# A hybrid decoder layer: seven block products for eight in the up-projection, and a down-projection of its own

## The chip, the cores and the metric

The kernel runs on one core of one Trainium2 chip. The metric is device time in microseconds (us) of one execution; the kernel before takes 2393.1 us (median of three runs, 2392.64 to 2393.7). Engines: PE does matmuls (PEld is its weight load), DVE is the vector engine, ACT the scalar engine, POOL is GpSimd and SP issues most DMA transfers (SPq, POOLq: their queues).

## What is computed

One layer on 2048 tokens of 1024 features. First a token-mixing part (retention, short convolution and an output projection), which the change leaves alone. Then the part that it rebuilds:

```python
h = modulate(rms_norm(x, norm2_g[layer]), shift2, scale2)
up = h @ w_up[layer]                    # 1024 -> 2 x 2816
a, val = up[..., :D_FF], up[..., D_FF:]
a = causal_dwconv(a, ffn_conv_w[layer]) + ffn_conv_b[layer]
ffn = (jax.nn.silu(a) * val) @ w_down[layer]     # 2816 -> 1024
x = x + gate2[:, None, :] * ffn
```

A last modulated norm gives the output. All tensors are float32.

## The kernel before

Features lie on the 128 partitions, tokens along the free dimension in blocks of 512 (four blocks; 8 feature chunks of 128). Every matmul operand is kept as two parts in the format fp32r, the rounded value and the rest (`split_act` at L217 for tokens, `split_w` at L83 for weights: an ACT cast, then a DVE subtraction). A product takes three matmuls for each 128 x 128 weight block (`mm3`, L235: value x value, value x rest, rest x value).

The token-mixing part runs over the four blocks. Its output projection (`out_proj`, L474) writes the residual x1 of each block to DRAM (`x1d`, stored by POOL's queue) and sums its squares; `norm2` (L497) turns the sum into the row `r2d`, also in DRAM. Between the steps of `out_proj` small jobs are placed by `spread` (L608): the next token chunks, and `more_mod` (L596), which reduces conditioning weights on DVE (L166). During the last output projection the 8 chunks of block 0 for the second part are made by `h2_chunk` (L684: load, a DVE multiplication, an ACT scaling, a split), and those of block 1 follow.

The second part works on 1024 tokens at a time (B = 0, 1; two blocks s). For each of 22 column chunks j of 128 it computes gate and value (`Up.a` L723, `Up.v` L739): 24 matmuls each into one of four PSUM banks `mm`, for each s. ACT copies the gate out of PSUM, then come the three-tap convolution (L731 to L733), Silu (L736), the product with the value (L744) and the split into g, which stays in SBUF. After every second j `down_part` (L752) multiplies two g chunks with two chunks of w_down and adds the result to the residual tiles `acc` in SBUF (L759), for 8 output chunks m and both s; the four PSUM banks sc0, sc1, y, misc take turns. At the end of B = 0 the last four chunks of the down-projection go in two groups, and after each m one token chunk of the next 1024 tokens is made (L866 to L874), so these lie between matmuls:

```python
for js in ((j - 3, j - 2), (j - 1, j)):
    ws = [get_w("w_down", q) for q in js]
    for m in range(KC):
        for s in range(2):
            down_part([gs[q] for q in js], ws, acc, s, m)
        if js[1] != j:
            hs[0].append(h2_chunk(2, m, r_s, new_xm()))
        else:
            hs[1].append(h2_chunk(3, m, r_t, new_xm()))
```

At the end of B = 1 the last four chunks go for blocks of 512, 256 and 256 tokens, so that the final norm and the stores (`Final`, L761) of one block lie beside the matmuls of the next; only the last 256 tokens are left behind the last matmul.

Each engine works through its queue in order. Outside `tc.manual_schedule()` the framework's planner sets the order of each queue: the instructions in the order of the program, but one that is not ready can be passed by later ones. Waits come from data and from buffers: a pool gives a tag a number of buffers (`bufs`), and a tile waits until the tile that had its buffer is done with. Weights are loaded through 3 raw buffers and split into 4 buffers, in the order of `plan` and up to `ahead` tiles early (`get_w`, L110).

## Time and profile before

| what | before |
|---|---|
| median of 3 runs | 2393.1 us |
| the profiled execution | 2391.5 us |
| its span, first to last instruction | 2389.7 us |
| PE busy | 2357.0 us (99%) |
| DVE busy | 1495.0 us (63%) |
| ACT busy | 838.1 us (35%) |
| moved by DMA | 239.5 MB, mean 100 GB/s |

The profile is that of one execution. Its span runs from the first to the last instruction and is 1.8 us shorter than that execution's time. Busy times overlap, as the engines work side by side. In rows by line, "mean ns" is what one instruction takes by itself; instructions of one engine follow each other a little closer than that, since the end of one overlaps the start of the next. "Clock" is the share of TensorE's full speed that was granted.

### The profile page before, as it was taken

The numbers are of one execution on the slowest core, as the hardware profiler recorded it, in microseconds if no ns is written. First come the engines' busy times: TensorE is split into PE (matmuls) and PEld (weight loads), VectorE is DVE, ScalarE is ACT, GpSimd is POOL, SyncE is SP. The second block draws the span as 40 slices with busy tenths as digits, with TensorE's granted clock in tenths as the row PEclk, the third lists the DMA queues.
The fourth block names the chain that finished last, engine by engine and source line by source line (L and its number), as shares of the span: only waits on it lengthen the run. The fifth ranks groups of instructions, "written<-read, shape, count | busy, mean of one in ns | idle before, by whom it ended". The sixth has DMA issues, their size and how long they took to land.

```text
span 2389.7 us, 27984 instructions
## 1 busy us (share of the span) xinstructions
PE 2357.0 (99%) x10954; PEld 1951.6 (82%) x10954; DVE 1495.0 (63%) x2755; ACT 838.1 (35%) x1234; POOL 32.0 (1%) x67
## 2 busy tenths in 40 slices
PE   8999999999999999999999999999999999999997
PEld 5888888888888887888888888888888888888887
DVE  8999759866986688644444444448844444444436
ACT  5255325523552355322222222235622222222234
POOL 0000000000000000000000000000100000000000
PEclk9999999999999999999999999999999999999998
DMA  8444633554264328311111111112511111111101
GB/s 308 144 132 135 230 111 112 175 189 150 71 217 153 115 84 271 103 53 53 40 50 53 53 39 50 53 53 72 189 58 45 44 53 53 44 45 53 53 27 71
DMA packets 88660, 239.53 MB, mean 100 GB/s; under 512 B 10240, under 2 KB 12304, under 8 KB 88528
## 3 DMA queue, kind: packets, MB, share of 16 engines
q1 hardware_dynamic: 84096, 223.71, 28.6%
q0 software_dynamic: 4288, 13.91, 1.5%
q8 instruction: 86, 1.41, 0.2%
q14 instruction: 46, 0.38, 0.0%
q10 hardware_dynamic: 144, 0.13, 0.0%
HBM read 219.88 MB, written 17.83 MB: 99 GB/s over the span
## 4 chain that ended last, share of the span: by engine, by line
PE 61%; issue 28%; DVE 6%; DMA 2%; ACT 1%; POOL 1%; SPq 0%; POOLq 0%; DVEq 0%; ACTq 0%
PE mm L237 14%; PE mm L238 14%; PE mm L239 14%; PE sc L239 3%; PE sc L238 3%; PE sc L237 3%; PE misc L237 2%; PE y L238 2%; PE y L239 2%; PE y L237 2%; PE misc L238 2%; PE misc L239 2%; DMA x<-in_x 1%; DVE mw L166 1%; DVE w L89 1%
## 5 line engine op out<-in xcount | busy, mean ns | idle before, releaser
L237 PE MATMUL mm<-act,w 128*128 128x512 f32 x2048 | 801.1, 391 | 1.3 <-DVE xr L492 1.1
L238 PE MATMUL mm<-act,w 128*128 128x512 f32 x2048 | 797.7, 389 | 1.0 <-DVE act L219 1.0
L239 PE MATMUL mm<-act,w 128*128 128x512 f32 x2048 | 797.3, 389 | 0.0
L88 ACT CAST w<-raw 128x1024 fp32r<-128x1024 f32 x271 | 282.9, 1051 | 656.6 <-issue 352.2
L237 PEld LDWEIGHTS mm<-act,w 128*128 128x128 f32 x2048 | 384.5, 188 | 81.4 <-ACT act L218 2.6
L238 PEld LDWEIGHTS mm<-act,w 128*128 128x128 f32 x2048 | 384.6, 188 | 80.7 <-DVE act L219 2.1
L239 PEld LDWEIGHTS mm<-act,w 128*128 128x128 f32 x2048 | 384.4, 188 | 80.4
L89 DVE TENSOR_TENSOR w<-raw,w 128x1024 fp32r<-128x1024 f32 x271 | 328.9, 1222 | 120.6 <-ACT w L88 120.6
L237 PE MATMUL mm<-w,act 128*128 128x512 f32 x480 | 187.9, 393 | 6.5 <-ACT act L218 3.6
L238 PE MATMUL mm<-w,act 128*128 128x512 f32 x480 | 188.0, 392 | 0.0
L239 PE MATMUL mm<-w,act 128*128 128x512 f32 x480 | 186.6, 391 | 0.0
L759 DVE SCALAR_TENSOR_TENSOR acc<-sc,mod,acc 128x512 f32<-128x512 f32 (+1 forms) x172 | 126.8, 738 | 76.7 <-PE sc L239 76.6
L732 DVE SCALAR_TENSOR_TENSOR fi<-a,cp,fi 128x512 f32<-128x512 f32 x88 | 66.1, 752 | 172.4 <-ACT fi L731 172.4
L744 DVE TENSOR_TENSOR fi<-fi,mm 128x512 f32<-128x512 f32 x88 | 60.5, 688 | 168.0 <-PE mm L239 167.3
L729 ACT COPY a<-mm 128x512 f32<-128x512 f32 x88 | 51.7, 588 | 315.2 <-PE mm L239 315.2
L238 PE MATMUL sc<-g,w 128*128 128x512 f32 (+1 forms) x348 | 132.9, 382 | 0.0
L237 PE MATMUL sc<-g,w 128*128 128x512 f32 (+1 forms) x348 | 132.8, 382 | 0.0
L239 PE MATMUL sc<-g,w 128*128 128x512 f32 (+1 forms) x348 | 132.8, 382 | 0.0
L237 PEld LDWEIGHTS mm<-w,act 128*128 128x128 f32 x480 | 90.0, 188 | 29.5 <-ACT act L218 9.6
L239 PEld LDWEIGHTS mm<-w,act 128*128 128x128 f32 x480 | 90.6, 189 | 19.3 <-DVE act L219 0.2
L238 PEld LDWEIGHTS mm<-w,act 128*128 128x128 f32 x480 | 90.7, 189 | 18.9 <-DVE w L542 0.5
L735 DVE COPY ah<-a 128x2 f32<-128x2 f32 x44 | 7.4, 169 | 156.2 <-ACT a L729 156.2
(226 smaller groups left out, 2812.9 us busy)
## 6 DMA issues: line engine op xcount, KB each, us to landing
raw<-in_w_up SPq DMA_DIRECT2D x88, 512.0 KB, 3.6
raw<-in_w_tok SPq DMA_DIRECT2D x64, 512.0 KB, 5.2
x<-in_mod_w SPq DMA_DIRECT2D x96, 256.0 KB, 4.1
raw<-in_w_conv SPq DMA_DIRECT2D x48, 512.0 KB, 3.5
raw<-in_w_down SPq DMA_DIRECT2D x44, 512.0 KB, 3.5
raw<-in_w_out SPq DMA_DIRECT2D x32, 512.0 KB, 3.5
x<-in_x SPq DMA_DIRECT2D x56, 256.0 KB, 3.9
mw<-in_mod_w SPq DMA_DIRECT2D x32, 256.0 KB, 4.6
```

Of the source, the lines that this page charges most:

```text
L88: S.copy(w[:, 0, :], raw)
L89: V.tensor_tensor(w[:, 1, :], raw, w[:, 0, :].bitcast(F32), op=ALU.subtract)
L166: V.scalar_tensor_tensor(raw, raw, 1.0, half, op0=ALU.mult, op1=ALU.mult, accum_out=part[:, q : q + 1])
L237: T.matmul(out, lhs[0], rhs[0], start=first, stop=False)
L238: T.matmul(out, lhs[0], rhs[1], start=False, stop=False)
L239: T.matmul(out, lhs[1], rhs[0], start=False, stop=last)
L729: S.copy(at[:, 2 + o : 514 + o], pa)
L732: V.scalar_tensor_tensor(cv, at[:, 1 + o : 513 + o], fcw[:, j, 1:2], cv, op0=ALU.mult, op1=ALU.add)
L735: V.tensor_copy(ah[:, j, :], at[:, 512 + o : 514 + o])
L744: V.tensor_tensor(sl, sl, pv, op=ALU.mult)
L759: V.scalar_tensor_tensor(acc[s][m][:, cs], ps, gate_of(1, m), acc[s][m][:, cs], op0=ALU.mult, op1=ALU.add)
```

## The change

The up-projection of 1024 tokens and of one column chunk pair (gate A, value V) is seen as a product of 2 x 2 blocks: the feature halves are 1 (chunks 0 to 3) and 2 (chunks 4 to 7), the token halves are the two blocks. Instead of eight block products, seven of combined operands are made (12 matmuls of 512 columns each, `product`). The combinations of tokens H11, H21, H12, H22 (feature half, token half) are made once for 1024 tokens, in four chunks (`Tokens`): T1 = H12 - H11, T2 = H22 - T1, T3 = H22 - H12, T4 = H21 - T2. Those of the weights are made for each column chunk (`Weights`), from the same loads.

A chunk's products are `start` (A1 H11 and A2 H21: the gate of token half 1), `middle` (with T2, T1 and T3) and `finish` (with T4 and H22). The products with H11, T2, T3 and T4 add up in one bank `pb`; after the first three ACT copies the bank (`snap`), and the copies are the partial sums that the other outputs need. `finish` of a chunk comes after `start` of the next one.

Gate times value is no longer kept in SBUF: POOL's queue writes it to DRAM (`gd`). When the up-projection of all tokens is done, a stage of its own does the down-projection for five token blocks of 512, 512, 512, 256 and 256: for each of 22 chunks it loads and splits the weights and g, and adds into eight PSUM banks, one for each output chunk m; m = 7 lags three chunks. At a block's end each bank is added to the residual, loaded then from `x1d`. The four token chunks for the first 1024 tokens are made in and after the last output projection (two of the `more_mod` jobs go from there to the convolution stage before it), those for the second 1024 tokens where the loop reaches i = 22. The memory of each stage's buffers is that of the stage before.

```diff
--- before.py
+++ after.py
...
+    base, wts = ExitStack(), ExitStack()
+    actp = base.enter_context(tc.tile_pool(name="actp", bufs=16))
+    fo = base.enter_context(tc.tile_pool(name="fo", bufs=4))
...
+    sp = wts.enter_context(tc.tile_pool(name="sp", bufs=7, side="right"))
+    whlp = wts.enter_context(tc.tile_pool(name="whlp", bufs=4, side="right"))
+    rawp = wts.enter_context(tc.tile_pool(name="rawp", bufs=3, side="right"))
...
-    for B in range(2):
-        for j in range(FC):
-            plan += [("w_up", j), ("w_up", FC + j)]
-            if j % 2 == 0 and 2 <= j < FC - 2:
-                plan += [("w_down", j - 2), ("w_down", j - 1)]
-            if j == FC - 1:
-                plan += [("w_down", q) for q in range(j - 3, j + 1)]
...
                 ret[j + 1].scores()
-                if j == 0:
+                if j == 0 or b == NB - 1:
                     more_mod()
...
+    p1.close()
+    p2 = ExitStack()
+    act2 = p2.enter_context(tc.tile_pool(name="act2", bufs=12, reuse_waits="tile"))
+    p3 = ExitStack()
+    hx = p3.enter_context(tc.tile_pool(name="hx", bufs=1, reuse_waits="tile"))
...
+    def h2_f32(b, k, r, t):
+        nc.sync.dma_start(t, x1d[b][k])
+        V.tensor_tensor(t, t, r, op=ALU.mult)
+        S.activation(t, t, AF.Identity, bias=shift_of(1, k), scale=amul[:, 1, k : k + 1])
+        return t
...
+        def chunk(self, i):
+            X, b, r = self.X, self.b, self.r
+            h11 = h2_f32(b, i, r[0], self.tmp())
+            X["11"].append(split_into(new_act(), h11))
+            h21 = h2_f32(b, i + 4, r[0], self.tmp())
+            X["21"].append(split_into(new_act(), h21))
+            h12 = h2_f32(b + 1, i, r[1], self.tmp())
+            h22 = h2_f32(b + 1, i + 4, r[1], self.tmp())
+            V.tensor_tensor(h11, h12, h11, op=ALU.subtract)
+            t2 = self.tmp()
+            V.tensor_tensor(t2, h22, h11, op=ALU.subtract)
+            X["T2"].append(split_into(new_x2(), t2))
+            X["T1"].append(split_into(new_x2(), h11))
+            V.tensor_tensor(h12, h22, h12, op=ALU.subtract)
+            X["T3"].append(split_into(new_x2(), h12))
+            t4 = self.keep() if self.keep else t2
+            V.tensor_tensor(t4, h21, t2, op=ALU.subtract)
+            if self.keep:
+                self.t4.append(t4)
+            else:
+                X["T4"].append(split_into(new_act(), t4))
+                X["22"].append(split_into(new_act(), h22))
+        def late(self, i):
+            self.X["T4"].append(split_into(new_act(), self.t4[i]))
+            self.X["22"].append(split_into(new_act(), h2_f32(self.b + 1, i + 4, self.r[1], self.tmp())))
...
+    tk = Tokens(0, [load_r2(0, new_hx("r", 2)), load_r2(1, new_hx("r", 2))], ft, lambda: new_hx("t4", 4))
+    ss2 = out_proj(3, mixed, spread(cv[3].norm, lambda k: tk.chunk(k) if k < 4 else None))
...
+    for i in range(4):
+        tk.late(i)
+    norm2(3, ss2)
+    p3.close()
+    pf.close()
+    wts.close()
+    p4 = ExitStack()
+    ap_ = p4.enter_context(tc.tile_pool(name="ap_", bufs=2, reuse_waits="tile"))
+    p4.enter_context(tc.tile_pool(name="sp3", bufs=7, side="right")).tile([128, 8], F32, tag="s", name="sp3")
+    whlp = p4.enter_context(tc.tile_pool(name="whlp2", bufs=5, side="right", reuse_waits="tile"))
+    rawp = p4.enter_context(tc.tile_pool(name="rawp2", bufs=4, side="right", reuse_waits="tile"))
...
+        def one(self):
+            self.a = self.new()
+            self.split(self.a, slice(0, 1024), self.wa)
+        def two(self):
+            wa, wv = self.wa, self.wv
+            lo, hi = slice(0, 512), slice(512, 1024)
+            s12 = rawp.tile([128, 1024], F32, tag="raw", name=nm("raw"))
+            V.tensor_tensor(s12[:, lo], wv[:, lo], wv[:, hi], op=ALU.add)
+            V.tensor_tensor(s12[:, hi], s12[:, lo], wa[:, lo], op=ALU.subtract)
+            self.s = self.new()
+            self.split(self.s, slice(0, 1024), s12)
+            self.b = self.new()
+            self.split(self.b, lo, wv[:, hi])
+            V.tensor_tensor(wv[:, lo], wa[:, lo], wv[:, lo], op=ALU.subtract)
+            V.tensor_tensor(wa[:, hi], wa[:, hi], s12[:, hi], op=ALU.subtract)
+            self.split(self.b, hi, wa[:, hi])
+        def three(self):
+            self.c = fo.tile([128, 2, 512], F32R, tag="q", bufs=1, name=nm("q"))
+            self.split(self.c, slice(0, 512), self.wv[:, 0:512])
+    def product(ps, w, c0, x, first):
+        for i in range(4):
+            cs = slice(c0 + 128 * i, c0 + 128 * (i + 1))
+            mm3(ps, [w[:, q, cs] for q in range(2)], [x[i][:, q, :] for q in range(2)], first and i == 0, i == 3, True)
 
...
+        def snap(self):
+            t = ft_o() if self.n % 2 else fo.tile([128, 512], F32, tag="xr", name=nm("sn"))
+            self.n += 1
+            S.copy(t, self.pb)
+            return t
+        def gate_branch(self, s, part, ps):
+            j, at, o = self.j, self.at, 512 * s
+            V.tensor_tensor(at[:, 2 + o : 514 + o], part, ps, op=ALU.add)
+            cv = new_ss() if s == 0 else fo.tile([128, 512], F32, tag="xr", name=nm("cv"))
+            S.activation(cv, at[:, 2 + o : 514 + o], AF.Identity, bias=fcb[:, j : j + 1], scale=fcw[:, j, 2:3])
+            V.scalar_tensor_tensor(cv, at[:, 1 + o : 513 + o], fcw[:, j, 1:2], cv, op0=ALU.mult, op1=ALU.add)
+            V.scalar_tensor_tensor(cv, at[:, o : 512 + o], fcw[:, j, 0:1], cv, op0=ALU.mult, op1=ALU.add)
+            if s == 1:
+                V.tensor_copy(ah[:, j, :], at[:, 512 + o : 514 + o])
+            S.activation(cv, cv, AF.Silu)
+            return cv
...
+            self.pb, self.pg = ps_tag(("sc0", "sc1")[j % 2]), ps_tag(("y", "misc")[j % 2])
+            product(self.pb, w.a, 0, X["11"], True)
+            s1 = self.snap()
+            pa = ps_mm()
+            product(pa, w.a, 512, X["21"], True)
+            self.sl0 = self.gate_branch(0, s1, pa)
+        def middle(self):
+            X, w = self.X, self.w
+            product(self.pb, w.s, 512, X["T2"], False)
+            self.u2 = self.snap()
+            product(self.pg, w.s, 0, X["T1"], True)
+            product(self.pb, w.c, 0, X["T3"], False)
+            self.v1 = self.snap()
+            V.tensor_tensor(self.v1, self.v1, self.pg, op=ALU.add)
+        def finish(self):
+            X, w, B, j = self.X, self.w, self.B, self.j
+            product(self.pb, w.b, 0, X["T4"], False)
+            V.tensor_tensor(self.sl0, self.sl0, self.pb, op=ALU.mult)
+            nc.gpsimd.dma_start(gd[2 * B][j], self.sl0)
+            product(self.pg, w.b, 512, X["22"], False)
+            sl1 = self.gate_branch(1, self.u2, self.pg)
+            V.tensor_tensor(sl1, sl1, self.v1, op=ALU.mult)
+            nc.gpsimd.dma_start(gd[2 * B + 1][j], sl1)
...
+    for i in range(2 * FC):
+        B, j = divmod(i, FC)
+        if i == FC:
+            last.finish()
+            last = None
+            turn = [0]
+            def tmp():
+                turn[0] += 1
+                return ft_o() if turn[0] % 2 else fo.tile([128, 512], F32, tag="xr", name=nm("h"))
+            tk = Tokens(2, [load_r2(2, new_ss()), load_r2(3, new_ss())], tmp)
+            for c in range(4):
+                tk.chunk(c)
+        w = nxt
+        u = Up(B, j, w, tk.X)
+        more = i + 1 < 2 * FC
+        if more:
+            nxt = Weights((j + 1) % FC)
+        u.start()
+        if more:
+            nxt.raw()
+            nxt.one()
+        if last is not None:
+            last.finish()
+        if more:
+            nxt.two()
+        u.middle()
+        if more:
+            nxt.three()
+        last = u
+    last.finish()
...
+    whlp, gp, rawp, grp = pool("whlp3", 6), pool("gp", 6), pool("rawp3", 3), pool("grp", 4)
+    accp, fo, sp = pool("accp", 18), pool("fo2", 4), pool("sp2", 8)
+    BANKS = ("mm", "mm", "mm", "mm", "sc0", "sc1", "y", "misc")
+    LAG = 3
...
+        def evict(self, ps, m):
+            t = accp.tile([128, 512], F32, tag="acc", name=nm("acc"))[:, 0 : self.n]
+            b, o = divmod(self.t0, 512)
+            nc.sync.dma_start(t, x1d[b][m][:, o : o + self.n])
+            V.scalar_tensor_tensor(t, ps, gate_of(1, m), t, op0=ALU.mult, op1=ALU.add)
+            self.acc.append(t)
...
+    for t0, n in ((0, 512), (512, 512), (1024, 512), (1536, 256), (1792, 256)):
+        b, o = divmod(t0, 512)
+        fin = Final(t0, n)
+        ws, gs = {}, {}
+        ps = [None] * KC
+        def part(m, k):
+            if k == 0:
+                ps[m] = ps_tag(BANKS[m])[:, 0:n]
+            mm3(ps[m], [ws[k][:, q, 128 * m : 128 * (m + 1)] for q in range(2)],
+                [gs[k][:, q, 0:n] for q in range(2)], k == 0, k == FC - 1)
+        for k in range(FC):
+            ws[k] = split_w(a["w_down"][k])
+            graw = grp.tile([128, 512], F32, tag="gr", name=nm("gr"))[:, 0:n]
+            nc.sync.dma_start(graw, gd[b][k][:, o : o + n])
+            gs[k] = gp.tile([128, 2, 512], F32R, tag="g", name=nm("g"))
+            split_act(gs[k][:, :, 0:n], graw)
+            for m in range(KC - 1):
+                part(m, k)
+                if k == FC - 1:
+                    fin.evict(ps[m], m)
+                    fin.sq(m)
+            if prev is not None and k == 0:
+                prev.out()
+            if k >= LAG:
+                part(KC - 1, k - LAG)
+        for k in range(FC - LAG, FC):
+            part(KC - 1, k)
+        fin.evict(ps[KC - 1], KC - 1)
+        if t0 + n < SEQ:
+            fin.sq(KC - 1)
+        prev = fin
+    prev.sq_last("sc0")
+    for m in range(KC):
+        prev.store(prev.r, m, nc.gpsimd if m in (2, 5) else nc.sync, m % 3 == 2)
```

## Rows read from the trace of the kernel before

**Rows 1.** The page's busy times: us, share of the span, instructions.
```profile
PE 2357.0 (99%) x10954; PEld 1951.6 (82%) x10954; DVE 1495.0 (63%) x2755; ACT 838.1 (35%) x1234; POOL 32.0 (1%) x67
```

**Rows 2.** Stretches: us, busy of PE, PEld, DVE, ACT, POOL, clock, DMA, GB/s.
```profile
1900.00:2300.00 400.00, 400.00 (x1766) 331.24 (x1765) 185.22 (x255) 96.53 (x134) 0.00 (x0) 1.00 0.15 48
...
200.00:700.00 500.00, 494.58 (x2437) 411.67 (x2436) 391.43 (x802) 223.89 (x336) 11.96 (x22) 1.00 0.47 153
```

**Rows 3.** Timeline of PE near the end, 256-wide down-projection: start us, us.
```profile
2371.95 0.28 PE L237 MATMUL misc<-g,w 128*128 128x256 f32 x1
...
2374.70 0.28 PE L239 MATMUL sc<-act,w 128*128 128x256 f32 x1
```

**Rows 4.** Groups by line and shape: busy us, mean ns, idle before.
```profile
L89 DVE TENSOR_TENSOR w<-raw,w 128x1024 fp32r<-128x1024 f32 x271 | 328.9, 1222 | 120.6 <-ACT w L88 120.6
L88 ACT CAST w<-raw 128x1024 fp32r<-128x1024 f32 x271 | 282.9, 1051 | 656.6 <-issue 352.2 <-PE mm L239 284.1 <-PE sc L239 16.2
...
L731 ACT ACTIVATE fi<-mm,cp 128x512 f32<-128x512 f32 x88 | 69.0, 784 | 0.0
...
L732 DVE SCALAR_TENSOR_TENSOR fi<-a,cp,fi 128x512 f32<-128x512 f32 x88 | 66.1, 752 | 172.4 <-ACT fi L731 172.4
...
L219 DVE TENSOR_TENSOR g<-fi,g 128x512 fp32r<-128x512 f32 x84 | 57.9, 689 | 26.5 <-ACT g L218 26.4
...
L736 ACT ACTIVATE fi<-fi 128x512 f32<-128x512 f32 x88 | 55.8, 634 | 96.7 <-DVE fi L733 96.5
L218 ACT CAST g<-fi 128x512 fp32r<-128x512 f32 x84 | 51.9, 618 | 103.7 <-DVE fi L744 103.5
L729 ACT COPY a<-mm 128x512 f32<-128x512 f32 x88 | 51.7, 588 | 315.2 <-PE mm L239 315.2
...
L735 DVE COPY ah<-a 128x2 f32<-128x2 f32 x44 | 7.4, 169 | 156.2 <-ACT a L729 156.2
```

**Rows 5.** DMA issues: count, KB each, median us to landing.
```profile
raw<-in_w_up SPq DMA_DIRECT2D x88, 512.0 KB, 3.6
raw<-in_w_tok SPq DMA_DIRECT2D x64, 512.0 KB, 5.2
...
x<-xr POOLq DMA_DIRECT2D x32, 256.0 KB, 5.0
...
x<-x SPq DMA_DIRECT2D x8, 256.0 KB, 3.5
...
ss<-r SPq DMA_DIRECT2D x4, 256.0 KB, 5.2
```

**Rows 6.** Last output projection: two stretches (columns as Rows 2), then timeline rows.
```profile
884.50:928.50 44.00, 44.00 (x195) 36.13 (x193) 36.91 (x70) 26.09 (x39) 2.17 (x4) 1.00 0.61 203
860.00:880.00 20.00, 20.00 (x103) 16.91 (x102) 17.35 (x41) 9.24 (x16) 0.00 (x0) 1.00 0.24 79
...
902.32 1.29 DVE L219 TENSOR_TENSOR act<-fo,act 128x512 fp32r<-128x512 f32 x2
...
912.23 0.69 DVE L166 SCALAR_TENSOR_TENSOR x<-x,cact 128x512 f32<-128x512 f32 x1
...
929.66 0.47 PE L237 MATMUL mm<-act,w 128*128 128x512 f32 x1 [1.06 <-DVE xr L492]
```

**Rows 7.** A stretch at the switch of token halves (columns as Rows 2).
```profile
1640.00:1660.00 20.00, 20.00 (x90) 16.57 (x89) 19.60 (x29) 14.03 (x22) 0.00 (x0) 1.00 0.22 66
```

**Rows 8.** A stretch at the kernel's start (columns as Rows 2).
```profile
14.00:16.00 2.00, 1.50 (x10) 0.95 (x9) 1.86 (x8) 0.00 (x0) 0.00 (x0) 1.00 1.06 408
```

**Rows 9.** Two stretches (columns as Rows 2) and PE's timeline within them.
```profile
22.00:24.00 2.00, 2.00 (x6) 1.31 (x5) 2.00 (x7) 0.16 (x1) 0.00 (x0) 0.55 0.95 290
24.00:26.00 2.00, 2.00 (x7) 1.54 (x7) 2.00 (x8) 0.00 (x0) 0.00 (x0) 0.60 0.85 284
...
24.14 0.63 PE L239 MATMUL mm<-w,act 128*128 128x512 f32 x1
24.57 0.63 PE L238 MATMUL mm<-w,act 128*128 128x512 f32 x1
```

267 lines of the change are left out of this document (76 added, 191 removed).

## The prediction

> **What bounds the kernel now.** I read the page's busy times first: PE is busy for 2357.0 us of 2389.7 us, the vector engine (DVE) 63%, the scalar engine (ACT) 35% [rows 1]. Busy time alone proves little for pipelined matmuls, so next I read the stretches: in 400 us of the feed-forward part 1766 matmuls of 128x512 start, one every 226.5 ns, at full clock, with no gap [rows 2]. That is the bound: in this part the time is the number of matmuls times their spacing. DVE and ACT have room there (46% and 24%). In the stretch 200 to 700 us, where DVE is 78% and ACT 45% busy, PE loses 5.4 of 500 us [rows 2].
>
> **Fewer matmuls.** One column chunk of gate and value on 1024 tokens takes 4 x 24 = 96 matmuls now, 7 x 12 = 84 after. There are 44 such chunks, so 528 matmuls go: 528 x 0.2265 = **-119.6 us** [rows 2]. All of it lies on the path, for PE has no gap.
> The Trainium skill (TensorE: Matmul & The Clock Gate, Back-to-back issue gap) gives a sustained spacing of about 131 ns for 512 columns with their weight loads; by it the cut would be worth 69 us, an estimate from that page, and the end would come 50 us later. The trace does not agree: the row's 226.5 ns stands for the same thing and decides.
>
> **Narrower matmuls.** The down-projection keeps its arithmetic, but two of its five token blocks are 256 wide: 2 x 22 x 24 = 1056 such matmuls against 192 now, 864 more. 23 intervals from 2371.95 to 2374.70 us give 119.6 ns each [rows 3], against half of 226.5 = 113.2: 864 x 6.4 ns = **+5.5 us**. The weight loads stay hidden.
>
> **The up stage, steady.** PE needs 84 x 0.2265 = 19.0 us per chunk. DVE gets two 1024-wide splits at 1.22, seven 512-wide adds and splits at 0.69, two gate branches (an add at 0.69, two multiply-adds at 0.75 each), three more 0.69 operations and two small copies: 14.1 us. ACT gets two casts at 1.05, three at 0.62, three snapshots at 0.59, two scalings at 0.78 and two Silus at 0.63: 8.5 us [rows 4]. Both are 74% and 45% of 19.0 us, the load of 200 to 700 us, where PE lost 1.1%; at 46% DVE load it lost nothing [rows 2]. Bounds 0 and 9 us of 837; I take half a per cent, **+4 us**. The two stores per chunk go through POOL's queue, 5.0 us to landing [rows 5], with nothing behind them inside the stage. Loads are 1 MB per 19 us on SP's queue, less than now: hidden by the 19 us of products.
>
> **Into the up stage.** The 16 old token chunks cost two DVE operations each, 8 of them inside the last output projection. Now four combination chunks of 13 operations (4 multiplies, 4 subtractions, 5 splits) and four late parts of 3 must pass. Independent 0.69 us operations start about 0.605 us apart (two in 1.29) [rows 6]. The projection, 884.5 to 928.5 us, keeps DVE busy for 36.9 us [rows 6]; off go 16 x 0.605 and 8 modulation reductions (8 x 0.69 = 5.5, moved to the convolution phase, whose DVE is 17 of 20 us busy [rows 6]), on come 52 x 0.605 = 31.5: 53 us of work in 44, ending at 938 with DVE never idle. It will idle: five scratch buffers hold one chunk, and each chunk's loads take 3.5 us [rows 5], so I say 943. Then come four late parts (7.3 us), evictions and squares (5 us): 955. The second raw weight of the first chunk lies in the memory of the scratch buffers, so only then come its load (3.6 us, [rows 5]), two adds, a cast and a split (1.3 + 1.05 + 1.22): about 962. PE, which today waits 1.06 us at 929.66 [rows 6], has start(0) (5.4 us) to do before; it then waits for the third product. 962 - 929.7 - 5.4 = 27; some of start(1) may fit. I take **+25 us**. Bounds: 3 (DVE full, weights in time: 938 against 935) and 40 (start(0) behind it all).
>
> **The switch to the second 1024 tokens.** Today it is hidden: in 1640 to 1660 us DVE is 19.6 us busy while PE has no gap, because the token chunks stand between down-projection groups [rows 7]. Those groups leave this place. Now 4 chunks x 15 DVE operations x 0.605 = 36.3 us stand between finish(21) and middle(22). Only eight scratch buffers (fo, xr) exist, so two chunks can begin early, with 4 operations each. The second row of norms needs the buffer of finish(21)'s first gate, whose store must land (5.0 us) before the row is loaded (5.2 us) [rows 5]: it is there 8 us after PE has ended finish(21). From there 2 x 11 x 0.605 + 9.1 + 5.4 us pass until the last T2 is split: 36 us. PE has start(22) and most of one product (8 us) meanwhile, perhaps start(23). **+27 us**; bounds 12 (DVE's 6.4 us of slack in the chunk before, start(23) and one product all used) and 44 (8 + 36.3, nothing overlapped).
>
> **Into the down stage.** All new buffers lie over those of the up stage. Raw weights and gates can be loaded when their old tiles are free, some with the last chain (gate branch 4.3 us, store 5.0 us), then 3.6 us landing and 2.3 us of splitting [rows 4, 5]. Bounds 0 and 16; nearest are the buffers free since the last start, so **+6 us**.
>
> **The down stage.** Per chunk of the sum PE takes 5.4 us (2.9 on half blocks), DVE 1.9 (1.6), so DVE is hidden. Weights are loaded five times, not twice: on half blocks 640 KB per 2.9 us = 223 GB/s, where the start of the kernel moved 408 [rows 8]. At a block's end eight evictions and squares (1.44 us each on DVE) stand against 7.5 us of PE work; the norm's sum waits for the last. Before the tail PE has 1.4 us less cover than DVE needs. Four boundaries at 1.5 and the tail at 2: **+8 us**, bounds 0 and 20.
>
> **The clock.** After a wait early in the kernel the granted clock was 0.55 and 0.60 for 4 us (the 1.2 GHz level) and matmuls stood 0.43 us apart [rows 9]. Two long waits: some 10 matmuls x 0.2 us each, **+4 us**, bounds 0 and 8.
>
> **Sum.** -119.6 + 5.5 + 4 + 25 + 27 + 6 + 8 + 4 = -40.1 us. The profiled execution took 2391.5 us (span 2389.7), 1.6 below the median of 2393.1: 2391.5 - 40.1 + 1.6 = about **2352 us**.
>
> **Rivals.**
> (a) The seams are filled: the order of each engine's queue lets the next chunk's products run while tokens are built, so each seam costs its lower bound. -119.6 + 5.5 + 3 + 12 + about 3 = -96: 2297 us. For it: today's order interleaves well and PE has almost no gap. Against it: at the switch the buffers, not the order, hold the work back.
> (b) Slower: the snapshots. Four products go into one bank, and the third of a bank's four may not start before ACT has copied the bank. Its only cover is one product, 12 x 0.2265 = 2.7 us. If ACT's queue has that copy behind weight casts (1.05, 0.62, 0.62) that wait for DVE, every chunk stalls. A stall of 2 us is 88 us: 2440. It decides from (2388 - 2352) / 44 = 0.8 us per chunk. For it: the copies of gate values stand in that queue between casts. Against it: ACT is 45% busy, and at this load today PE loses 1.1%.
> (c) The half blocks are bound by weight buffers: three raw buffers, each held for issue 0.3, landing up to 5.2 (busy row, [rows 5]), cast 1.05 and split 1.22, some 7.8 us, or 2.6 per chunk against PE's 2.9. With queueing at 9.6 us it is 3.2: 44 x 0.3 = 13 us more, 2365.
> (d) The change does nothing on balance, within 0.2%: only if seams take all of the gain, 2393.
>
> **How the numbers follow.** Forecast 0.57, (a) 0.22, (b) 0.10, (c) 0.08, (d) 0.03. All lower bounds together give 2294, all upper ones 2416. The forecast's own range is 2315 to 2388; with half of (a) below and (b) above left out, 2304 to 2392. A measurement of this kernel tells about 0.2% from no change, 2388 to 2398. Faster: forecast, (a) and (c), 0.87; same 0.03; slower, (b), 0.10.
>
> **What would show it.** PE's count down by 528 matmuls of 512 and their spacing still 226 ns; about 837 us for the up stage outside the seams; waits of PE's loads on DVE splits of the combined tokens, some 20 to 30 us each, near 935 and in the middle of the up stage; DVE near 74% between. Wrong would be: a wait of PE on the bank's copy in every chunk (b), a wait on raw weights throughout the last 130 us (c), or seams of a few us (a).

## The result, and the profile after

The changed kernel takes 2355.5 us (median of 4 runs, 2352.8 to 2357.7); the kernel before takes 2393.4 us on the same chip (2392.6 to 2394.6). The ratio is **0.9841, 95% interval 0.9824 to 0.9858**: 38 us less, where the prediction's last line said 2352 us, 41 less. Times are medians of the executions at the usual clock: one execution of the version with an early w_down block took 2855.9 us, at a mean granted clock of 0.75, and is left out. The profiled execution took 2353.7 us, its span 2351.6 us against 2389.7.

The page's busy times, which answer to [rows 1], and two of its rows of 40 slices:

```profile
PE 2261.1 (96%) x10838; PEld 1881.4 (80%) x10838; DVE 1651.2 (70%) x3033; ACT 1033.2 (44%) x1536; POOL 87.9 (4%) x171
...
PE   8999999999999998699999989999999799999997
...
PEclk9999999999999999899999989999999899999999
```

PE is no longer busy throughout: its slices have three dips, at 940, 1400 and 1840 us. Those are the three seams of the prediction: into the up stage, to the second 1024 tokens, into the down stage. Three stretches between the seams, then four at and around them (us, busy of PE, PEld, DVE, ACT, POOL, clock, DMA share, GB/s):

```profile
1000.00:1300.00 300.00, 300.00 (x1326) 248.40 (x1325) 202.65 (x317) 130.22 (x190) 17.26 (x32) 1.00 0.25 84
1500.00:1800.00 300.00, 300.00 (x1325) 248.52 (x1324) 201.07 (x313) 128.94 (x188) 17.27 (x32) 1.00 0.24 81
1900.00:2200.00 300.00, 300.00 (x1324) 248.42 (x1324) 139.15 (x175) 114.66 (x156) 8.64 (x16) 1.00 0.50 166
...
900.00:960.00 60.00, 35.72 (x140) 26.89 (x138) 56.25 (x91) 37.68 (x61) 4.32 (x8) 0.85 0.47 159
960.00:980.00 20.00, 18.05 (x71) 14.38 (x72) 18.72 (x26) 11.80 (x17) 0.54 (x1) 0.86 0.33 92
...
1350.00:1450.00 100.00, 86.36 (x338) 65.34 (x338) 87.14 (x140) 59.58 (x92) 4.31 (x8) 0.91 0.32 106
...
1780.00:1870.00 90.00, 74.99 (x319) 61.24 (x318) 36.00 (x50) 27.00 (x39) 3.78 (x7) 0.91 0.46 164
```

Between the seams nothing is lost: 1324 to 1326 matmuls start in 300 us, one every 226 to 227 ns as before [rows 2], with DVE at 68% and ACT at 43% in the up stage. At the seams the count of matmuls tells the loss: 338 in 100 us at the switch, where 441 fit (100 / 0.2265): 103 x 0.2265 = 23.4 us. In 13.6 of the 100 us PE is idle; the rest of the loss is matmuls at a lower clock (granted 0.91 over the stretch).
The 131 ns of the Trainium skill (TensorE: Matmul & The Clock Gate, Back-to-back issue gap) are not met by this trace either.

What PE waited for from 900 us on (engine and line, released by; us in total, times, longest):

```profile
PE mm L233 <- ACT g L214: 14.9, 2, 14.3
PE misc L178 <- ACT q L214: 9.7, 1, 9.7
PE sc L233 <- ACT w L777: 8.5, 1, 8.5
PE mm L233 <- ACT act L214: 5.5, 1, 5.5
PE mm L233 <- DVE xr L489: 5.2, 2, 2.6
...
PE sc L233 <- ACT sn L817: 1.0, 2, 0.7
```

PE's timeline (start us, us, idle before it and what ended that): two waits and the last product of the last output projection, the first product of the up stage, the first behind the wait at the switch and the first of the down stage:

```profile
918.61 0.50 PE L233 MATMUL mm<-act,w 128*128 128x512 f32 x1 [2.59 <-DVE xr L489]
...
924.68 0.74 PE L233 MATMUL mm<-act,w 128*128 128x512 f32 x1 [2.57 <-DVE xr L489]
...
939.71 0.39 PE L235 MATMUL mm<-act,w 128*128 128x512 f32 x1
...
961.95 0.79 PE L233 MATMUL sc<-act,w 128*128 128x512 f32 x1 [8.51 <-ACT w L777]
...
1390.70 1.22 PE L233 MATMUL mm<-act,w 128*128 128x512 f32 x2 [5.52 <-ACT act L214]
...
1840.93 1.65 PE L233 MATMUL mm<-g,w 128*128 128x512 f32 x3 [14.34 <-ACT g L214]
```

**Where the 38 us come from.** The up stage starts at 961.95 us; before, PE's first product of the feed-forward part was at 929.66 [rows 6]. That is 32.3 us later, and 11.5 of these had arisen by the end of the last output projection: PE was done with it at 940.1 (939.71 + 0.39), before at 928.6 (929.66 - 1.06), and its two waits on evictions (L489), 5.2 us, with the clock of 0.83 from 920 to 930 us, are some 7 us of that. The up stage ends at 1840.93 - 14.34 = 1826.6, so it takes 864.6 us. The 44 x 84 matmuls need 837.1 of these; 27.5 are lost: 23.4 at the switch, 1.9 to the half clock just behind the first wait (27 matmuls in the 8.05 us to 970, where 35.5 fit), and 2.2 that I could not place. In the down stage 43 matmuls start from 1840.93 to 1853 us, 2.3 us of these 12.1 are lost to the half clock (granted 0.50 up to 1846). The rest of that stage loses 7.6 us (495.0 us from 1840.93 to 2335.9, less 485.1 us of matmuls, less these 2.3), and the tail is 0.8 longer. The kernel before took more than its matmuls in its feed-forward part: 1445.2 us (929.66 to 2374.8) for 6240 x 0.2265 + 192 x 0.1196 = 1436.3 us of matmuls. These 8.9 us end with it. Term by term, in us, added up before rounding:

| term | forecast (bounds) | measured |
|---|---|---|
| fewer matmuls | -119.6 | -119.6 |
| narrower matmuls | +5.5 | +5.5 |
| steady up stage | +4 (0 to 9) | 0 |
| into the up stage | +25 (3 to 40) | +32.3 |
| switch | +27 (12 to 44) | +23.4, its half clock with it |
| into the down stage | +6 (0 to 16) | +14.3 |
| down stage and tail | +8 (0 to 20) | +8.4 |
| clock elsewhere | +4 (0 to 8) | +4.3 |
| time beyond matmuls, kernel before | not in the sum | -8.9 |
| not placed | | +2.2 |
| sum | -40.1 | -38.1 |

### The profile page after: what moved, and what is told of

The parts are those of the page before. It is cut to its first block, busy times and chain, and to the rows that moved or that the text cites. A ratio compares the mean times of both kernels' runs of the same rounds, so it can differ in the third digit from the quotient of the medians.

```text
span 2351.6 us, 29468 instructions
## 1 busy us (share of the span) xinstructions
PE 2261.1 (96%) x10838; PEld 1881.4 (80%) x10838; DVE 1651.2 (70%) x3033; ACT 1033.2 (44%) x1536; POOL 87.9 (4%) x171
## 4 chain that ended last, share of the span: by engine, by line
issue 65%; PE 23%; DVE 5%; POOL 3%; DMA 2%; ACT 1%; SPq 0%; POOLq 0%; DVEq 0%; ACTq 0%
PE mm L235 4%; PE mm L234 4%; PE mm L233 4%; PE sc L235 2%; PE sc L234 2%; PE sc L233 2%; POOL g L858 1%; DMA x<-in_x 1%; POOL g L862 1%; PE y L235 1%; PE y L234 1%; PE y L233 1%; DVE w L92 1%; PE misc L233 1%; PE misc L235 1%
## 5 line engine op out<-in xcount | busy, mean ns | idle before, releaser
L92 DVE TENSOR_TENSOR w<-raw,w 128x1024 fp32r<-128x1024 f32 x249 | 303.6, 1221 | 328.0 <-ACT w L91 327.6
L91 ACT CAST w<-raw 128x1024 fp32r<-128x1024 f32 x249 | 261.4, 1050 | 478.3 <-PE misc L235 208.8
L233 PE MATMUL mm<-act,w 128*128 128x512 f32 x816 | 324.2, 398 | 10.7 <-ACT act L214 5.5
L234 PE MATMUL mm<-act,w 128*128 128x512 f32 x816 | 319.7, 392 | 0.1
L235 PE MATMUL mm<-act,w 128*128 128x512 f32 x816 | 318.4, 392 | 0.8 <-DVE w L92 0.8
L233 PE MATMUL sc<-act,w 128*128 128x512 f32 x528 | 207.0, 393 | 13.7 <-ACT w L777 8.5
L777 ACT CAST w<-raw 128x1024 fp32r<-128x1024 f32 (+1 forms) x176 | 143.0, 836 | 151.6 <-PE mm L235 81.8
L234 PE MATMUL sc<-act,w 128*128 128x512 f32 x528 | 207.2, 392 | 1.3 <-DVE act L215 1.2
L235 PE MATMUL sc<-act,w 128*128 128x512 f32 x528 | 207.0, 392 | 0.0
L778 DVE TENSOR_TENSOR w<-raw,w 128x1024 fp32r<-128x1024 f32 (+1 forms) x176 | 167.3, 956 | 41.6 <-ACT w L777 41.5
L233 PEld LDWEIGHTS mm<-act,w 128*128 128x128 f32 x816 | 154.5, 189 | 43.3 <-DVE xr L489 6.3
L235 PEld LDWEIGHTS mm<-act,w 128*128 128x128 f32 x816 | 154.0, 189 | 34.3 <-DVE w L92 1.5
L234 PEld LDWEIGHTS mm<-act,w 128*128 128x128 f32 x816 | 154.4, 189 | 31.8 <-DVE act L215 1.0
L233 PE MATMUL mm<-g,w 128*128 128x512 f32 (+1 forms) x440 | 150.8, 350 | 15.3 <-ACT g L214 14.9
L234 PE MATMUL mm<-g,w 128*128 128x512 f32 (+1 forms) x440 | 153.2, 350 | 1.4 <-DVE g L215 1.2
L235 PE MATMUL mm<-g,w 128*128 128x512 f32 (+1 forms) x440 | 153.0, 349 | 0.8 <-DVE w L92 0.8
L233 PEld LDWEIGHTS sc<-act,w 128*128 128x128 f32 x528 | 99.5, 189 | 37.3 <-ACT w L777 9.0
L823 DVE TENSOR_TENSOR a<-sn,mm 128x512 f32<-128x512 f32 x44 | 30.3, 688 | 141.0 <-PE mm L235 140.9
L234 PEld LDWEIGHTS sc<-act,w 128*128 128x128 f32 x528 | 99.9, 189 | 23.4 <-DVE act L215 2.9
```

The lines of the kernel that those rows point to most:

```text
L91: S.copy(w[:, 0, :], raw)
L92: V.tensor_tensor(w[:, 1, :], raw, w[:, 0, :].bitcast(F32), op=ALU.subtract)
L233: T.matmul(out, lhs[0], rhs[0], start=first, stop=False, skip_group_check=on)
L234: T.matmul(out, lhs[0], rhs[1], start=False, stop=False, skip_group_check=on)
L235: T.matmul(out, lhs[1], rhs[0], start=False, stop=last, skip_group_check=on)
L777: S.copy(w[:, 0, cs], src)
```

## The experiments

My theory was the prediction's: the up stage is bound by PE alone, and what is lost is lost at three seams, each for a reason of its own. Rivals were, for the whole, waits spread over the stage, and for each seam another thing that releases it: the memory that a load waits for, the order in an engine's queue, or an engine's total work. Gains of the versions below are read from matmul counts of the seam's stretch and from the span beside 2351.6; the ratios are to the kernel before, on one chip per group of runs.

**Is PE the bound?** One more product for each chunk, into a bank that nobody reads.

```diff
             product(self.pb, w.s, 512, X["T2"], False)
             self.u2 = self.snap()
+            product(ps_mm(), w.s, 0, X["T2"], True)
```

> Added: an eighth product per column chunk, 12 matmuls into a bank that nobody reads (44 x 12 = 528 matmuls). Theory P: the up stage is bound by PE alone, so all of it shows, less what it fills of the gaps at the seams: 2355.5 + 119.6 - 0 to 8 = 2467 to 2475 us. Rival D: a chunk's period is set by DVE, ACT or the waits on the bank copies, and PE has hidden slack: under 2450 us.

One run took 2469.4 us, its span 2467.6: 116 us more than the changed kernel for 528 x 0.2265 = 119.6 us of matmuls. PE is the bound; an eighth product would cost its full price. That also says that the -119.6 us are had in full.

**What is the switch worth?** The parts of the second 1024 tokens are not made.

```diff
-            tk = Tokens(2, [load_r2(2, new_ss()), load_r2(3, new_ss())], tmp)
-            for c in range(4):
-                tk.chunk(c)
```

> Left out: the token combinations of the second 1024 tokens are not made, the second half runs on those of the first. This takes the switch away. Theory: the switch costs 23 us of PE (gaps and half clock), nothing else hangs on it: 2330 to 2336 us, and one matmul every 226.5 ns from the start of the up stage to its end. If the switch's DVE work also slowed products outside it, the gain is over 30 us; if other waits (weights, stores) take its place, under 12 us.

2329.4 us, ratio 0.9723 (0.9708 to 0.9737); the span is 23.7 us shorter, and the stretch of the switch has no gap:

```profile
1300.00:1450.00 150.00, 150.00 (x663) 124.05 (x663) 100.86 (x157) 64.54 (x95) 8.67 (x16) 1.00 0.26 85
```

So the 23.4 us counted above are this work's price. DVE's timeline in the changed kernel says what kind of price it is: its operations follow one another 0.60 us apart, from

```profile
1387.75 0.68 DVE L700 TENSOR_TENSOR fo<-fo,ss 128x512 f32<-128x512 f32 x1
...
1420.59 0.68 DVE L726 TENSOR_TENSOR h<-fo,h 128x512 f32<-128x512 f32 x1
```

on, 33 us with a single idle time of 1.34. Four experiments tell whether it is DVE's total work or an order.

**The switch, subtractions on GpSimd.** Lines 721, 723, 726 and 729, the first of them shown; the edit holds for the token chunks of both halves:

```diff
-            V.tensor_tensor(h11, h12, h11, op=ALU.subtract)
+            G.tensor_tensor(h11, h12, h11, op=ALU.subtract)
...
```

> The four token subtractions of each chunk (T1, T2, T3, T4 before their splits; 32 in all, 16 of them at the switch) are issued on GpSimd and not on VectorE. Theory V (at the switch to the second 1024 tokens VectorE's own work sets the pace: it runs nearly without idle for 33 us with operations 0.60 us apart): 16 operations x 0.6 us leave it, the switch gets shorter by 6 to 10 us, and the end of the last out projection, where evictions queue behind the same work, by 0 to 4; ratio 0.979 to 0.982. Rival P (the chain load, multiply, scale, split sets the pace, or GpSimd needs so much longer for a subtraction that it takes VectorE's place): no gain at the switch or up to 10 us lost; ratio 0.984 to 0.988.

2369.5 us, ratio 0.9895 (0.988 to 0.991): slower than the changed kernel, by more than the rival's worst case. The stretch of the switch holds 302 matmuls and not 338 (8.2 us lost), that from 900 to 980 us 177 and not 211 (7.7 us). Both engines lose. DVE's costliest groups from 1400 to 1440 us (count, busy us, mean ns of one):

```profile
L215 DVE TENSOR_TENSOR act<-h,act 128x512 fp32r<-128x512 f32 x13 | 12.0, 961 | 3.2 <-ACT act L214 3.2
L215 DVE TENSOR_TENSOR act<-fo,act 128x512 fp32r<-128x512 f32 x12 | 11.9, 1021 | 0.1
```

and rows of GpSimd's and of DVE's timeline there:

```profile
1411.09 2.63 POOL L721 TENSOR_TENSOR h<-h,h 128x512 f32<-128x512 f32 x1 [4.48 <-ACT h L701]
...
1421.61 1.67 POOL L721 TENSOR_TENSOR fo<-fo,fo 128x512 f32<-128x512 f32 x1 [3.04 <-DVE act L215]
...
1422.06 1.77 DVE L215 TENSOR_TENSOR act<-h,act 128x512 fp32r<-128x512 f32 x1
```

A subtraction takes 1.3 to 2.6 us there, and a DVE operation of 0.68 us beside one takes up to 1.77. The Trainium skill (SBUF — State Buffer, Who interferes with whom) says that a DVE instruction with two SBUF inputs contends with a GpSimd instruction that reads SBUF, and that the one that comes second is blocked, not slowed. The trace agrees: the two kinds are what met here, and DVE's operation of 1422.06 ends at 1423.83, 0.55 us behind GpSimd's subtraction (1421.61 + 1.67 = 1423.28), as if it had waited for that to end. Work moved between these two engines was not work removed here; whether DVE's total work or an order sets the switch is not tested by this run.

**The switch, parts 11 and 21 made early.** They go ahead of finish(21); their inputs are loaded and scaled twice for that.

```diff
-            tk = Tokens(2, [load_r2(2, new_ss()), load_r2(3, new_ss())], tmp)
+            tk = Tokens(2, [load_r2(2, new_ss())], tmp)
+            for c in range(4):
+                tk.first(c)
             last.finish()
...
             for c in range(4):
-                tk.chunk(c)
+                tk.rest(c)
```

> Parts 11 and 21 of the second 1024 tokens are made ahead of the last five products of the first half (from the rows of the second, whose load is moved up), the other parts behind finish(21) as before; the two inputs are loaded and scaled a second time for that (8 loads, 8 multiplications and 8 scalings more). Theory H (the switch is VectorE and ScalarE work that stood behind finish(21) and can lie under its products): VectorE works through 2 + 2 operations of each of the four chunks while TensorE has its 5.4 to 13.6 us of products; 8 to 14 us less at the switch; ratio 0.978 to 0.981. Rival W (the work of the token parts delays gate branches and the weights' second group instead, so that TensorE waits there, or the parts that are left set the end): 0 to 4 us less; ratio 0.982 to 0.985.

2355.6 us, ratio 0.9839 (0.9823 to 0.9856): nothing. The stretch from 1350 to 1450 holds 337 matmuls against 338. PE goes on to 1398 without a long wait and then has the waits that it had before, with DVE full:

```profile
1380.00:1390.00 10.00, 10.00 (x43) 8.07 (x44) 9.96 (x18) 8.30 (x14) 0.54 (x1) 1.00 0.60 202
...
1400.00:1410.00 10.00, 3.35 (x7) 1.72 (x7) 10.00 (x18) 6.98 (x12) 0.00 (x0) 0.73 0.53 163
1410.00:1420.00 10.00, 6.05 (x12) 3.26 (x12) 10.00 (x18) 6.88 (x11) 0.00 (x0) 0.50 0.32 105
```

An earlier start buys little: DVE's steady load leaves 32% of the 14 us of products in question, about 4.5 us, and the second multiplications take as much (8 x 0.6 us, an estimate). The rival holds, which speaks for DVE's total work.

**The switch, subtractions left out.**

The kernel splits other parts of the same shape in place of T1 to T4; one of the four is shown.

```diff
-            V.tensor_tensor(h11, h12, h11, op=ALU.subtract)
...
+            if self.keep:
+                V.tensor_tensor(h11, h12, h11, op=ALU.subtract)
...
```

> The sixteen subtractions that make T1, T2, T3 and T4 of the second 1024 tokens are left out (these parts are split from 11, 22, 12 and 21 instead, so the second half's products take wrong operands of the same shape). Theory V (VectorE's total work at the switch sets its length: making parts early and moving subtractions to GpSimd, at 1.3 to 2.6 us each, gained nothing because neither made that work less): 16 x 0.6 = 9.6 us less work, 7 to 10 us less time; ratio 0.980 to 0.9815. Rival L (the load, the multiplication, the scaling and the split of one chunk after the other set it, with the queues of ScalarE and the row's load): 0 to 3 us less; ratio 0.983 to 0.985.

2345.6 us, ratio 0.9792 (0.9778 to 0.9805). The switch is shorter by (364 - 338) x 0.2265 = 5.9 us; the medians say 0.49%, 11.7 us, the spans 4.6. Between these, the work theory's 7 to 10 is nearer than the rival's 0 to 3, but 9.6 us of DVE work gave back only some 6 in the stretch. With it gone ACT is busy for 9.4 of 10 us from 1400 to 1410 (7.7 before), so its casts probably begin to count; this was not tested further.

**The switch, parts worked out ahead.** In twelve iterations of the first half (3 to 14) a step of two or three operations of DVE makes some of the unsplit parts and puts them into DRAM; the switch only loads and splits them.

```diff
+        if 3 <= i < 15:
+            if i == 3:
+                nt = Tokens(2, None, None)
+            if i in (3, 7):
+                nt.row = load_r2(3 if i == 3 else 2, rhp.tile([128, 512], F32, tag="r", name=nm("r")))
+            nt.prep(i - 3)
...
-                tk.chunk(c)
+                tk.get("11", c, new_act)
+            for c in range(4):
+                tk.get("21", c, new_act)
+            last.finish()
+            last = None
+            for name in ("T2", "T1", "T3"):
+                for c in range(4):
+                    tk.get(name, c, new_x2)
...
```

> The 28 parts of the second 1024 tokens are worked out unsplit in twelve steps of the first half's up stage (VectorE is busy 68% there), put into DRAM, and only loaded and split at the switch, the first eight of them ahead of finish(21). Theory V (VectorE's work behind start(21) is the price of the switch): of 48 operations before the splits none is left there, 28 splits of 0.6 to 0.7 us are, some 18 us in place of 33, and eight of them lie under finish(21): 10 to 16 us less; ratio 0.977 to 0.980. Rival D (28 loads, 7.3 MB, take the place of VectorE's work, or the steps slow the steady stage): 0 to 4 us less, or longer; ratio 0.982 to 0.987.

2339.4 us, ratio 0.9766 (0.9752 to 0.9779): 17.2 us off the span. The stretch of the switch, in the kernel without the subtractions:

```profile
1350.00:1450.00 100.00, 87.70 (x364) 68.43 (x363) 82.58 (x132) 61.91 (x98) 4.85 (x9) 0.97 0.37 119
```

and with the parts worked out ahead, the stretch before it first:

```profile
980.00:1350.00 370.00, 370.00 (x1634) 306.47 (x1633) 266.56 (x422) 171.54 (x249) 38.33 (x71) 1.00 0.38 131
1350.00:1450.00 100.00, 96.04 (x417) 77.31 (x416) 81.23 (x128) 55.26 (x88) 5.36 (x10) 1.00 0.46 148
```

417 matmuls against 338: 79 x 0.2265 = 17.9 us less, and the steps cost the first half nothing (1634 matmuls, as before). DVE's work between start(21) and middle(22) was the price of the switch; taken to where DVE has room, it costs nothing that the counts show. (DVE is busy for 72% of the stretch before, 68% without the steps.)

**The seam into the up stage, memory.** The two pools change places, so that the first raw weights no longer lie over the scratch buffers.

```diff
-    whlp = p4.enter_context(tc.tile_pool(name="whlp2", bufs=5, side="right", reuse_waits="tile"))
     rawp = p4.enter_context(tc.tile_pool(name="rawp2", bufs=4, side="right", reuse_waits="tile"))
+    whlp = p4.enter_context(tc.tile_pool(name="whlp2", bufs=5, side="right", reuse_waits="tile"))
```

> The raw-weight buffers of the up stage are placed over the old weight buffers instead of over the token scratch buffers (two lines change places). Theory M (memory): the first products of the up stage wait because the first raw weight may only be loaded when the last late token part has left the scratch buffers (issue at 953.55 us, first product at 961.95). Freed from that, the load is issued near 930 us and the first product starts when the last token chunk's H21 is split, near 938 to 945 us; the next three products still wait for DVE's late parts and weight sums, so the gain is 5 to 15 us: 2340 to 2350 us. Rival W (work): DVE has so much to do at this place that the order and the memory do not matter; start and time stay, 2353 to 2358 us.

2353.2 us, ratio 0.9816 (0.9799 to 0.9832); the span, 2351.9, is that of the changed kernel, so a gain is not sure. The loads are issued 15 us earlier, and the first product starts where it did; the stretch from 900 to 980 us holds 220 matmuls against 211, 2.0 us. SyncE's queue and PE's timeline:

```profile
938.38 0.33 SPq L770 DMA_DIRECT2D raw<-in_w_up  x1
946.73 0.42 SPq L771 DMA_DIRECT2D raw<-in_w_up  x1
...
962.13 0.80 PE L233 MATMUL sc<-act,w 128*128 128x512 f32 x1 [5.16 <-ACT w L777]
```

In the changed kernel that first load went out at 953.55. It was late, but not what held the stage: the cast of line 777 stands in ACT's queue behind the late parts and the norm.

**The seam into the up stage, order.** The first weight block is loaded and cast ahead of the late parts and of norm2(3). The exchange of the pools is in this version too, and one row and the late parts' temporaries lie in other buffers.

```diff
     nxt.raw()
     nxt.one()
+    for i in range(4):
+        tk.late(i)
+    norm2(3, ss2)
...
```

> At the end of the last out projection the first weight block of the up-projection is loaded and cast ahead of the late token parts (T4 and 22) and of the second norm's last row; for this one row moves to another buffer, and the late parts' temporaries to another pool. Theory Q (start(0), whose first product is at 962 us in the changed kernel, waits in ScalarE's and VectorE's queues, where its casts stand behind the late parts that only finish(0) needs): first product at 945 to 952, 9 to 15 us less; ratio 0.977 to 0.980. Rival M (the evictions of the last out projection and the token parts themselves take this long, whatever the order): the late parts are then missing at finish(0), first product no earlier than 957, at most 4 us less; ratio 0.982 to 0.985.

2348.6 us, ratio 0.9811 (0.9794 to 0.9827), span 2346.1.

```profile
946.50 0.79 PE L233 MATMUL sc<-act,w 128*128 128x512 f32 x1 [4.48 <-ACT w L772]
...
962.24 0.80 PE L233 MATMUL sc<-act,w 128*128 128x512 f32 x1 [5.89 <-ACT w L772]
```

The first product starts 15 us earlier, as the order theory said; but the gain is 243 matmuls against 211 from 900 to 980 us, 7.2 us, not 9 to 15. The rest returns at 962.24, where the next product's weights now stand behind the late parts. The order set the start, together with the exchange, which alone had not moved it. What is left goes with DVE's total work (9.6 of 10 us busy, 910 to 990); that this sets the end is argued, not tested.

**The seam into the down stage, memory.** The pool of the split gates (gp) goes behind that of the residual, so raw weights and loaded gates (rawp, grp) lie over other tiles.

```diff
-    whlp, gp, rawp, grp = pool("whlp3", 6), pool("gp", 6), pool("rawp3", 3), pool("grp", 4)
-    accp, fo, sp = pool("accp", 18), pool("fo2", 4), pool("sp2", 8)
+    whlp, rawp, grp = pool("whlp3", 6), pool("rawp3", 3), pool("grp", 4)
+    accp, gp, fo, sp = pool("accp", 18), pool("gp", 6), pool("fo2", 4), pool("sp2", 8)
```

> In the down stage the buffers of raw weights and loaded gates are placed over token operands of the up stage, and the g buffers further up; nothing else changes. Theory S (store): PE's wait of 14.3 us before the down stage is the landing of the up stage's last store (6.0 us in SP's queue), because a buffer for loaded gates lies over that store's source, and then a load, a cast and a split. With other memory the loads wait for PE's last products only: the wait falls to 3 to 8 us, the time to 2344 to 2350 us. Rival L (latency): loading, casting and splitting the first weights and gates takes that long wherever they lie, or SP's queue is held up by the residual loads (10.8 us for 17 of them): the wait stays above 11 us, the time at 2353 to 2358 us.

2357.7 us, ratio 0.9839 (0.9824 to 0.9853): the same time. The wait became 11.5 us (first row), and what ended it changed: in the changed kernel the first gate load goes out at 1837.62, behind the last store; here it goes out behind a raw load that waits for a split, with three casts behind the last gate branch.

```profile
1843.49 1.65 PE L233 MATMUL mm<-g,w 128*128 128x512 f32 x3 [11.47 <-ACT g L214]
...
1835.80 2.92 ACT L91 CAST w<-raw 128x1024 fp32r<-128x1024 f32 x3
...
1838.11 0.33 SPq L89 DMA_DIRECT2D raw<-in_w_down  x1
1838.49 1.90 SPq L986 DMA_DIRECT2D gr<-g  x4
```

**The seam into the down stage, order.** The first w_down block is loaded and cast ahead of finish(43), in the up stage's weight buffers, which the down stage keeps; the gate blocks' buffers come first in the new memory.

```diff
+    w0 = split_w(a["w_down"][0])
     last.finish()
...
-    whlp, gp, rawp, grp = pool("whlp3", 6), pool("gp", 6), pool("rawp3", 3), pool("grp", 4)
+    grp, gp = pool("grp", 4), pool("gp", 6)
```

> The first block of w_down is loaded and cast ahead of finish(43) in the up-projection's own weight buffers, which the down-projection keeps (5 and 4 of them, not 6 and 3), and the gate blocks' buffers are the first of the new memory. Theory Q (the 14.3 us wait at the seam into the down stage is the place of the first cast and of the first gate loads in the queues of ScalarE and SyncE): 8 to 13 us less there; ratio 0.9785 to 0.981. Rival S (the first gate block can't come before the last store of the up stage has landed and its memory is free, 6 us behind the store's issue): 0 to 4 us less; ratio 0.982 to 0.9845. Fewer weight buffers could cost the steady down stage up to 5 us.

2345.4 us (median of three), ratio 0.98 (0.9783 to 0.9816), span 2343.6. The waits from 1780 to 1900 us:

```profile
PE mm L233 <- ACT g L214: 2.4, 1, 2.4
```

14.3 us have become 2.4, and with the half clock gone the stretch from 1780 to 1870 holds 379 matmuls, not 319: 13.6 us less. The span is only 8.0 shorter. PE's waits on splits of weights in the down stage (line 92) grow from 0.8 us to 3.8, probably because it has one buffer for split weights fewer; and the two other seams, which the edit does not touch, hold 5 and 9 matmuls fewer (206 for 211 from 900 to 980 us, 329 for 338 at the switch), 3.2 us.

**Together.** The edits of both order experiments, and then these with the parts worked out ahead (where two small buffers had to make room: uh moved to the attention stage's pool, a placeholder pool went).

> The first weight block ahead of the late token parts and the first w_down block ahead of finish(43), together. If the two seams are separate stretches, the gains of the two alone add up (span 5.5 and 8.0 us shorter): span 2337 to 2340, ratio 0.977 to 0.979. If one takes from the other, or the down stage's fewer weight buffers cost again: ratio 0.980 or more.

> The two seams and the token parts worked out ahead, together. By theory V 10 to 16 us less than with the two seams alone: span 2322 to 2329, ratio 0.970 to 0.974. By rival D no better than the two seams alone: ratio 0.977 or more.

Both seams: 2338.4 us, ratio **0.9763 (0.975 to 0.9776)**, span 2334.8: the gains add up, and this beats the changed kernel by 0.8%. All three: 2338.8 us, ratio 0.9762 (0.9749 to 0.9776), no more. Yet all three seams are short in its trace (421 matmuls in the switch's stretch, 374 at the down seam). The time went elsewhere, in a part that no edit was meant to touch. PE in the attention stage with both seams, a stretch (us, busy, clock, DMA share, GB/s):

```profile
450.00:470.00 20.00, 20.00 (x90) 1.00 0.67 226
```

and two of its groups from 200 to 800 us:

```profile
L234 PE MATMUL mm<-act,w 128*128 128x512 f32 x394 | 153.6, 390 | 0.0
L234 PE MATMUL mm<-w,act 128*128 128x512 f32 x384 | 149.5, 389 | 0.0
```

With all three, the same stretch, the same groups, and one row of PE's timeline:

```profile
450.00:470.00 20.00, 20.00 (x87) 1.00 0.58 191
```

```profile
L234 PE MATMUL mm<-act,w 128*128 128x512 f32 x397 | 157.7, 397 | 0.0
L234 PE MATMUL mm<-w,act 128*128 128x512 f32 x369 | 145.7, 395 | 0.0
```

```profile
951.08 0.73 PE L235 MATMUL mm<-act,w 128*128 128x512 f32 x2 [0.69 <-DVE w L92]
```

The last row's wait stands at 935.72 in the version with both seams: the attention stage is 15.4 us longer. Its clock is 1.00 in this stretch and PE waits no longer than before (idle for 26.7 us up to the first product of the up stage, 32.6 with both seams); its matmuls start 230 to 233 ns apart and not 226.5. PE and DVE have the same instructions in the same order there in both. What differs, by the order of the pools in the program, is that moving the 32 bytes of uh put the activations' buffers, and all behind them, 32 bytes lower, while the weights' buffers of that stage stayed. Without this the third version's span would be near 2321.6 us, an estimate (2337.0 - 15.4); it was not run.

## Why the prediction was right, and where it was not

The time (2352 against 2355.5) and the mechanism hold: the matmuls fell by 528 at an unchanged spacing, and some three fifths of their worth (70.0 of 119.6 us) are lost at the three seams. That the sum is so near is in part luck: the seams took 12.0 us more than the 58 forecast, and 8.9 us that the sum left out and 4 that it did not need took this back. The last step of the sum is also one off: 2391.5 - 40.1 + 1.6 is 2353.0, not 2352.

- **Fewer and narrower matmuls.** Right in full: 226 to 227 ns, and half matmuls 0.12 us apart in the changed kernel's timeline, as in [rows 3]. The added product confirms the price from the other side.
- **The up stage, steady.** DVE at 68% (forecast 74%), ACT at 43% (45%); nothing was lost where I took 4 us, though [rows 2]'s second stretch lost 1.1% with DVE at 78%. At 72%, with the parts worked out ahead, nothing was lost either, so load alone probably did not make the loss there. Rival (b), a wait on the bank's copy in every chunk, is out: two waits, 1.0 us in all.
- **Into the up stage.** Mis-sized, 32.3 for 25, since two steps failed. PE was to be free at 929.7 as before; it ended the last output projection at 940.1, as DVE, 88 to 94% busy from 910 to 930 us, was late with that projection's evictions. And "PE, which today waits 1.06 us at 929.66 [rows 6], has start(0) (5.4 us) to do before": start(0) itself was last: its load went out at 953.55 and its cast at 960.87, behind the late parts and the norm's chain. It was my upper bound, "start(0) behind it all". That a raw weight lies over the scratch buffers was seen right and mattered little (the exchange of the pools); that they stand behind work which nobody needs yet was not seen.
- **The switch.** 23.4 for 27, by the right mechanism: DVE's work, 33 us of it where I worked out 36.3. The late row, a step of that term, was not the hold: its load went out at 1384.74 us, as PE ended finish(21), and landed at most 3.8 us later, not 8 behind; DVE had four operations per chunk to do meanwhile, and no operation of the switch waited for it. The sign that I gave, waits of 20 to 30 us on DVE's splits, did not come: the longest wait is 5.5 us, on a cast of ACT, and the loss is spread over short waits and matmuls at the lower clock. Rival (a) held that today's order would fill this seam. It can't, for the work is too long, not badly ordered; put into the first half it fills it.
- **Into the down stage.** Mis-sized, 14.3 for 6. I took the value near "the buffers free since the last start"; the far end of 16, with the last chain in full, was the case. The experiments show both halves of that chain, the last store behind which the gate load waited and the casts behind the last gate branch; only when both were taken away did the wait go. The early cast without the other memory was not run.
- **Down stage and clock.** 8.4 for 8 and 4.3 for 4. The 4.3 is only what the half clock cost behind the two long waits; in the switch and in the last output projection it fell too, and the table has that in their terms. Rival (c), half blocks held by raw weights, is out in the changed kernel: waits of 2.9 us in the 256-wide blocks, not 13.
- **Left out of the sum.** The time that the kernel before took beyond its matmuls in the feed-forward part. I had read its stretches as free of gaps; over 1445 us it comes to 8.9 us, which the change takes away and which paid for most of what two seams took beyond the forecast.

## What to carry to other kernels

When a change cuts the work of the engine that bounds a kernel, price the seams by the other engines' total work there, and look in each queue for what stands ahead of the first thing the next stage needs: a buffer that comes free earlier gains little while the cast behind it waits for work that is needed later. Work that is too long for its seam is not helped by a better order, or by a second engine that holds up the first as GpSimd did here; put it where the busy engine has room, even through DRAM. After moving buffers, compare the spacing of the same instructions in stages that were not touched.

## What the runs showed of the hardware that was not expected

- DVE and GpSimd hold each other up: a 128x512 operation of DVE with both inputs in SBUF went from 0.68 us to 0.96 and 1.02 on average, at most 1.78, beside GpSimd's subtractions of the same size, which took 1.3 to 2.6 us.
- A 128x512 matmul of two 32-bit operands started every 226.5 ns, or every 230 to 233 ns (90 or 87 in 20 us) when the one operand's buffers lay 32 bytes off their old place and the other's did not. In the up stage of that same version, where the weights' buffers had moved too, by 224 bytes, it was 226.7 again (1632 in 370 us). One version showed it, and moving the buffers alone was not tried: the address is the only difference found, not a cause shown by itself.
- Behind the 14.3 us wait, and behind waits of 9.7, 2.0 and 8.5 us with one matmul between each, the granted clock fell to its lower level of 1.2 GHz (0.50 from 1840 to 1846, 0.77 on average from 962 to 970), and about 2 us were lost each time. Shorter waits were followed by it too: 0.50 from 1390 to 1400 us, behind the 5.5 us wait, and 0.83 from 920 to 930 us, behind two waits of 2.6 us. Where the 14.3 us wait became 2.4, the clock of the stretch stayed at 1.00.
